# A decoder layer on one core: the weight products of cross-attention formed in the first stage

## Chip, core and metric

The kernel runs on one core of one Trainium2 chip. The metric is the time of one execution on the device, in microseconds (us), as the median of several runs. The core has a matrix engine (PE, which also loads its stationary operand), VectorE (DVE), ScalarE (ACT), GpSimd (POOL) and SyncE (SP, which here does nothing but issue transfers). Each has a queue of its own and runs it in order.

## What is computed

One decoder layer on 1024 tokens of width 1024: a token-mixing sub-layer (RWKV-7 and sparse attention side by side), cross-attention into 256 memory rows, and a gated feed-forward part, each followed by a residual sum and a layer norm. The change touches the second:

```python
def memory_cross_attention(x, mem, wq, wk, wv, wo):
    q = (x @ wq).reshape(B, S, X_HEADS, X_HEAD_DIM)      # 4 heads of 256
    k = (mem @ wk).reshape(B, M, X_HEADS, X_HEAD_DIM)    # 256 memory rows
    v = (mem @ wv).reshape(B, M, X_HEADS, X_HEAD_DIM)
    s = jnp.einsum('bhsd,bmhd->bhsm', q, k) * X_HEAD_DIM ** -0.5
    pr = jax.nn.softmax(s, axis=-1)
    o = jnp.einsum('bhsm,bmhd->bshd', pr, v).reshape(B, S, D_MODEL)
    return o @ wo
```

(axes reordered for reading). Since `q k^T = x (wq k^T)`, the product of `wq` with a head's keys can be formed without `x`; likewise `v wo` without the softmax.

## The kernel before

All arithmetic is in float32, each operand split into a high part and a low rest (`split`, lines 199 to 201: ScalarE copies the high part, VectorE subtracts), and each product is three PE products (`mm3`, lines 194 to 197). Weights come through `wload` (lines 211 to 229): units of 128 x 1024 numbers, 512 KB, go into a tile `raw` (one buffer in each pool) and are split into `wh` and `wl` (two buffers in each pool). In the first stage the two pools `wa` and `p0` take turns, so two units can be on their way and four can be held split.

First stage, in program order: the projection `nsa_proj(512, 512)`, then `mem_T` (the memory transposed and split), `mem_k(0)`, `mem_v(0)`, `windows` (reads back part of the projection, `ev`), `nsa_proj(1024, 280)`, `compress` (two weights of 2 units each), `mem_k(1)`, `windows`, `mem_v(1)`, `compress`, `mem_k(2)`, `nsa_proj(0, 512)`, `mem_v(2)`, `mem_k(3)`, `mem_v(3)`. `mem_k(j)` multiplies 256 columns of `xa_wk` with the memory and stores 2 tiles in a scratch tensor `kscr`; `mem_v` does the same for `vscr`. The projection copies each result tile to `nst` by ScalarE, GpSimd rotates some columns (lines 355 to 358), and SP stores it to `rawn` (line 359). All copies of this kind share four buffers (`stt`).

After that stage the weight pool is `wa` alone, for the RWKV part, whose first products are called `prj`. Cross-attention comes later: `x_query(h)` forms a head's queries (`xq`) and splits them, `kscr` and `vscr` are read back and split (`kvld`), `x_front` forms scores (`xs`) and softmax, `x_back` transposes the probabilities (`xpt`) and multiplies with the values (`xo`), and `out_proj` multiplies with `xa_wo` (`op`), adds the residual and normalises. Large tiles go into two pools by the letters of `PLAN` (m or a). The framework orders the instructions of each engine when it builds the kernel, by readiness and by program order, so that neighbours in the program can change places.

Of the kernel before, what the change touches and what calls it, by code (L numbers as in the profile page):

```python
# [10 lines left out]
F32 = mybir.dt.float32  # L11
# [31 lines left out]
PSPLIT = "ggv"  # L43
FILL = (1, 0.9, 0.95, 0.95, 0.95, 0.95, 0.95, 0.95)
FILL0 = 1
PLAN = "mmmmmmmm" "aaaa" "a" "aaaammmm" "mmmmaaaa" "aaaa" "aa" "mmmmaama" "mmaa" "a" "maaammmm" + "aaaam" * 5
LAG = 3
GT = 8
XQ = 3
L_DENSE = 0.69  # L50
L_SUBST = 42
L_BACK = 7
# [74 lines left out]
def layer_kernel(ctx: ExitStack, tc, I, out, cst):  # L127
# [22 lines left out]
    def stt(shape, dt=F32, name="st"):  # L150
        return cur["st"].tile(shape, dt, tag="st", name=name, bufs=cur["nst"])
# [188 lines left out]
    def nsa_proj(cc, n, scale, nb, nh, w=None, ahead=lambda tt: None):  # L340
        w = w or wload([win[:, NSA0 + cc:NSA0 + cc + n]])
        for tt in range(NT):
            ahead(tt)
            ps = pg("np")
            gemmN(ps[:, :n], xT, tt, w, 0, n)
            t = stt([P, HALF], name="nst")
            S.activation(t[:, :n], ps[:, :n], AF.Copy, scale=scale)
            v = t[:, 0:256 * nb].rearrange("p (b h d) -> p b h d", h=4, d=64)[:, :, 0:nh, 0:16]
            for z in range(nb):
                vz = v[:, z]  # L350
                co = cso[:, tt * 16:tt * 16 + 16]
                si = cso[:, P + tt * 16:P + tt * 16 + 16]
                a = p0.tile([P, nh, 16], F32, name="rpa", tag="rpa", bufs=2)
                b = p0.tile([P, nh, 16], F32, name="rpb", tag="rpb", bufs=2)
                G.tensor_tensor(a, vz, bc(co, nh), op=OP.mult)
                G.tensor_tensor(b[:, :, 0:8], vz[:, :, 8:16], bc(si[:, 0:8], nh), op=OP.mult)
                G.tensor_tensor(b[:, :, 8:16], vz[:, :, 0:8], bc(si[:, 8:16], nh), op=OP.mult)
                G.tensor_tensor(vz, a, b, op=OP.add)
            SP.dma_start(rawn[tt * P:(tt + 1) * P, cc:cc + n], t[:, :n])

    rows_h = [slice(0, 64), slice(64, 128)]

# [79 lines left out]
                ms = slice(mt * P, mt * P + P)  # L442
                split(pt, memh[:, kh * 4:kh * 4 + 4, ms], meml[:, kh * 4:kh * 4 + 4, ms])

    def mem_k(j):
        w = wload([I["xa_wk"][0][:, j * 256:(j + 1) * 256]])
        for q in range(2):
            ps = pg("mk")
            for k in range(8):
                mm3(ps[:, :MEM], *w.at(k, q * P, P), memh[:, k], meml[:, k], k == 0, k == 7)  # L450
            t = stt([P, MEM], name="mks")
            S.activation(t, ps[:, :MEM], AF.Copy)
            SP.dma_start(kscr[j * 256 + q * P:j * 256 + q * P + P, :], t)

    def mem_v(j):
        w = wload([I["xa_wv"][0][:, j * 256:(j + 1) * 256]])
        for mt in range(2):
            ms = slice(mt * P, mt * P + P)
            ps = pg("mv")
            for k in range(8):  # L460
                mm3(ps[:, :256], memh[:, k, ms], meml[:, k, ms], *w.at(k, 0, 256), k == 0, k == 7)
            t = stt([P, 256], name="mvs")
            S.activation(t, ps[:, :256], AF.Copy)
            SP.dma_start(vscr[ms, j * 256:(j + 1) * 256], t)
# [24 lines left out]
    V.tensor_scalar(hbias, pv[:, c0:c0 + 8], 0.5, None, op0=OP.mult)  # L489

    mem_T()
    mem_k(0)
    mem_v(0)
    blocks = windows(512, "nsa_pe_k")
    nsa_proj(1024, 280, 1.0, 1, 2)
    compress(*blocks, "nsa_ck_w1", "nsa_ck_w2", True)
    mem_k(1)
    blocks_v = windows(640, "nsa_pe_v")
    mem_v(1)
    compress(*blocks_v, "nsa_cv_w1", "nsa_cv_w2", False)  # L500
    mem_k(2)
    nsa_proj(0, 512, 0.125, 2, 4)
    mem_v(2)
    mem_k(3)
    mem_v(3)


    gq = list(range(16))
# [836 lines left out]
            SP.dma_start(acc[i], src[i * 256:(i + 1) * 256, :].rearrange("(a p) d -> p a d", p=P))  # L1345
        return acc

    def out_proj(a, wname, res, gname, bname, dst=None, order=range(NT)):
        acc = residual(res, [tt // 2 for tt in order[::2]])
        norm = layer_norm(acc, gname, bname, dst)  # L1350
        nT = Act(b8, "nT")

        def add(w, j, tt):
            ps = pg("op")
            gemmN(ps, a, tt, w, 0, HALF)
            v = acc[tt // 2][:, tt % 2, j * HALF:(j + 1) * HALF]
            V.scalar_tensor_tensor(v, v, ALPHA, ps, op0=OP.mult, op1=OP.add)

        cols = lambda j: wload([I[wname][0][:, j * HALF:(j + 1) * HALF]])
        w = cols(0)  # L1360
        for tt in order:
            add(w, 0, tt)
        w = cols(1)
        rows = []
        for tt in range(NT + LAG):
            if tt < NT:
                add(w, 1, tt)
            if tt >= LAG:
# [6 lines left out]
    x1T, _ = out_proj(mT, "mix_w_o", x, "ln1_g", "ln1_b", x1, order=(4, 5, 6, 7, 0, 1, 2, 3))


    qh = [b8([P, 2, T], F32R, f"xqh{h}") for h in range(4)]
    ql = [b8([P, 2, T], F32R, f"xql{h}") for h in range(4)]
    def x_query(h):  # L1380
        w = wload([I["xa_wq"][0][:, h * 256:(h + 1) * 256]])
        for half in range(2):
            for q in range(2):
                ps = pg("xq")
                gemmT(ps, w, q * P, x1T, half)
                hs = slice(half * HALF, (half + 1) * HALF)
                split(ps, qh[h][:, q, hs], ql[h][:, q, hs])

    def x_front(h, half):
        ps = []  # L1390
        for q2 in range(2):
            s = pss("xs").rearrange("p (q m) -> p q m", m=MEM)
            for q in range(2):
                ts_ = slice((half * 4 + 2 * q2 + q) * P, (half * 4 + 2 * q2 + q + 1) * P)
                for k in range(2):
                    mm3(s[:, q], qh[h][:, k, ts_], ql[h][:, k, ts_], km[0][:, 2 * h + k], km[1][:, 2 * h + k], k == 0, k == 1)
            nm = sm.tile([P, 4], F32, name="xnm", tag="xnm", bufs=3)
            V.tensor_reduce(nm[:, 0:2], s, axis=AX.X, op=OP.max)
            V.tensor_scalar(nm[:, 0:2], nm[:, 0:2], -X_SCALE, None, op0=OP.mult)
# [6 lines left out]
        return ps  # L1406

    def x_back(h, half, ps):
        PT = []
        for mt in range(2):  # L1410
            pt = pst("xpt").rearrange("p (a t) -> p a t", t=P)
            for q in range(4):
                PE.transpose(pt[:, q, :], ps[q // 2][:, q % 2, mt * P:(mt + 1) * P], ident)
            PT.append([stt([P, HALF], F32R, name="xPT") for _ in range(2)])
            split(pt.rearrange("p a t -> p (a t)"), *PT[mt])
        for q in range(2):
            ps = pg("xo")
            for mt in range(2):
                ds_ = slice(h * 256 + q * P, h * 256 + q * P + P)
                mm3(ps, vm[0][:, mt, ds_], vm[1][:, mt, ds_], *PT[mt], mt == 0, mt == 1)  # L1420
            k = 2 * h + q
            split(ps, oT.h[half][k // 4][:, k % 4, :], oT.l[half][k // 4][:, k % 4, :])

    pend = []
    for h in range(XQ):
        x_query(h)
        if h == 0:
            kvh = [b8([P, 2048], F32R, f"kvh{i}") for i in range(2)]
            kvl = [b8([P, 2048], F32R, f"kvl{i}") for i in range(2)]
            for i in range(2):  # L1430
                t = b8([P, 2048], name="kvld")
                if i == 0:
                    SP.dma_start(t.rearrange("p (a m) -> p a m", m=MEM), kscr.rearrange("(a p) m -> p a m", p=P))
                else:
                    SP.dma_start(t.rearrange("p (a d) -> p a d", d=D), vscr.rearrange("(a p) d -> p a d", p=P))
                split(t, kvh[i], kvl[i])
            km = [kvh[0].rearrange("p (a m) -> p a m", m=MEM), kvl[0].rearrange("p (a m) -> p a m", m=MEM)]
            vm = [kvh[1].rearrange("p (a d) -> p a d", d=D), kvl[1].rearrange("p (a d) -> p a d", d=D)]
            oT = Act(b8, "oT")
# [12 lines left out]
    wup, wdn = I["ffn_w_up"][0], I["ffn_w_down"][0]
# [13 lines left out]
    for n in (2, 4, 4, 4, 4, 4):  # L1466
# [68 lines left out]
```

## Time and profile before

| | us |
|---|---|
| median of 3 runs (2221.66 to 2224.29) | 2224.1 |
| the profiled execution, its own time | 2223.49 |
| its span, first to last instruction | 2221.7 |
| PE busy with products | 2131.7 (96%) |
| VectorE busy | 1232.4 (55%) |
| ScalarE busy | 889.2 (40%) |
| GpSimd busy | 475.0 (21%) |

Busy shares are averages over stages with different limits. A record of a PE product overlaps the next ones, so a busy PE is not PE at its peak: the distance between starts tells the rate. A row of the timeline gives start, duration, engine, line, operation, output and inputs; what stands in brackets at its end is the idle time before it and what ended that. L195, L196 and L197 are the three products of `mm3`, L200 and L201 the two halves of a split, L224 the load of a weight unit, and SPq is SP's queue.

### The profile page before, as it was taken

What the parts mean: (1) busy time and instruction counts of PE and PEld (TensorE: products, weight loads), DVE (VectorE), ACT (ScalarE), POOL (GpSimd) and SP (SyncE); (2) the same over time, 40 slices, a digit from 0 to 9 for tenths busy, and PEclk for the clock granted to TensorE, in tenths of its full rate; (3) what the DMA queues carried; (4) which work ended last, traced back from release to release, by engine and by line L of the source; (5) the groups of instructions that cost most, each with busy time, mean ns of one, the idle gap of its engine ahead of it and who ended that gap; (6) DMA issues with size and microseconds to landing.
All of it is one profiled execution on the core that took longest, in us unless ns stands there. A gap on an engine that the chain in (4) does not pass through costs nothing.

```text
span 2221.7 us, 31651 instructions
## 1 busy us (share of the span) xinstructions
PE 2131.7 (96%) x12301; PEld 1706.0 (77%) x12301; DVE 1232.4 (55%) x2416; ACT 889.2 (40%) x1441; POOL 475.0 (21%) x544
## 2 busy tenths in 40 slices
PE   9989999999999899999899999999999999999997
PEld 7978777777778667756678877788888888888886
DVE  3422576777652787888656535275444434344447
ACT  3433443544533576776523424142322313132232
POOL 2112231333300244444422101030100101000013
PEclk9999999999999999999999999999999999999999
DMA  6544112121223321112252313111111111111102
GB/s 206 152 150 124 49 24 56 36 52 32 62 59 94 110 66 45 42 45 68 72 189 86 123 38 114 39 39 57 38 48 48 54 42 57 39 57 57 57 29 86
DMA packets 196659, 157.91 MB, mean 71 GB/s; under 512 B 49061, under 2 KB 164766, under 8 KB 196510
## 3 DMA queue, kind: packets, MB, share of 16 engines
q1 hardware_dynamic: 184798, 139.10, 21.2%
q10 hardware_dynamic: 11136, 14.68, 2.0%
q0 software_dynamic: 576, 2.10, 0.3%
q8 instruction: 98, 1.61, 0.3%
q14 instruction: 51, 0.42, 0.1%
HBM read 125.86 MB, written 29.98 MB: 70 GB/s over the span
## 4 chain that ended last, share of the span: by engine, by line
PE 47%; DVE 5%; ACT 2%; DMA 1%; issue 1%; POOL 0%; SPq 0%; ACTq 0%; DVEq 0%; POOLq 0%
PE up L196 7%; PE up L197 7%; PE up L195 7%; PE dn L195 4%; PE dn L197 4%; PE dn L196 4%; PE op L195 2%; PE op L197 1%; PE op L196 1%; PE xq L195 1%; PE xq L196 1%; PE xq L197 1%; DVE acc L1334 1%; ACT acc L1333 1%; DVE bs L1327 1%
## 5 line engine op out<-in xcount | busy, mean ns | idle before, releaser
L200 ACT ACTIVATE wh<-raw 128x1024 fp32r<-128x1024 f32 (+1 forms) x160 | 168.8, 1055 | 474.9 <-PE dn L197 138.1
L201 DVE TENSOR_TENSOR wl<-raw,wh 128x1024 fp32r<-128x1024 f32 (+1 forms) x160 | 198.1, 1239 | 282.5 <-ACT wh L200 281.5
L196 PE MATMUL up<-nTl,wh 128*128 128x512 f32 x704 | 276.5, 393 | 0.0
L197 PE MATMUL up<-nTh,wl 128*128 128x512 f32 x704 | 276.4, 393 | 0.0
L195 PE MATMUL up<-nTh,wh 128*128 128x512 f32 x704 | 276.4, 393 | 0.0
L1458 DVE SCALAR_TENSOR_TENSOR cv<-up,pv,cv 128x511 f32<-128x511 f32 (+1 forms) x176 | 131.5, 747 | 145.4 <-ACT cv L1456 143.4
L1482 POOL TENSOR_TENSOR cv<-cv 128x512 f32<-128x512 f32 x44 | 56.8, 1291 | 630.9 <-DVE cl L1462 413.5
L196 PEld LDWEIGHTS up<-nTl,wh 128*128 128x128 f32 x704 | 132.3, 188 | 29.6
L195 PEld LDWEIGHTS up<-nTh,wh 128*128 128x128 f32 x704 | 132.2, 188 | 29.6
L197 PEld LDWEIGHTS up<-nTh,wl 128*128 128x128 f32 x704 | 132.2, 188 | 29.6
L1106 POOL TENSOR_TENSOR pl<-pe,ph 128x512 fp32r<-128x512 f32 x87 | 114.3, 1317 | 161.3 <-ACT ph L1105 97.3
L195 PE MATMUL dn<-wh,gT 128*128 128x512 f32 x352 | 138.1, 393 | 0.2 <-ACT wh L200 0.2
L197 PE MATMUL dn<-wh,gT 128*128 128x512 f32 x352 | 137.5, 391 | 0.0
L196 PE MATMUL dn<-wl,gT 128*128 128x512 f32 x352 | 136.9, 389 | 0.0
L1493 DVE SCALAR_TENSOR_TENSOR acc<-acc,dn 128x512 f32<-128x512 f32 x96 | 65.5, 686 | 95.5 <-PE dn L197 94.9
L1456 ACT ACTIVATE cv<-up,pv 128x512 f32<-128x512 f32 x88 | 68.5, 778 | 117.2 <-PE up L197 117.2
L195 PE MATMUL gt<-xTh,wh 128*128 128x512 f32 x256 | 113.0, 441 | 0.5 <-DVE nm L1074 0.5
L197 PE MATMUL gt<-xTh,wl 128*128 128x512 f32 x256 | 102.3, 399 | 0.0
L196 PE MATMUL gt<-xTl,wh 128*128 128x512 f32 x256 | 101.9, 398 | 0.0
L1335 POOL TENSOR_TENSOR acc<-acc,lngb 128x1024 f32<-128x1024 f32 x21 | 50.4, 2401 | 206.0 <-DVE acc L1334 129.8
L1105 ACT ACTIVATE ph<-pe 128x512 fp32r<-128x512 f32 (+1 forms) x148 | 90.2, 627 | 6.9 <-POOL macc L1223 4.6
L195 PE MATMUL prj<-xTh,wh 128*128 128x512 f32 x208 | 90.5, 435 | 2.2 <-ACT wh L200 2.2
(365 smaller groups left out, 5092.2 us busy)
## 6 DMA issues: line engine op xcount, KB each, us to landing
raw<-in_ffn_w_up_dram SPq DMA_DIRECT2D x88, 256.0 KB
raw<-in_w_in_dram SPq DMA_DIRECT2D x33, 512.0 KB
raw<-in_ffn_w_down_dram SPq DMA_DIRECT2D x22, 512.0 KB
gscr<-gst ACTq DMA_DIRECT2D x32, 256.0 KB
rawn<-nst SPq DMA_DIRECT2D x16, 256.0 KB
raw<-in_xa_wk_dram SPq DMA_DIRECT2D x8, 512.0 KB
raw<-in_xa_wv_dram SPq DMA_DIRECT2D x8, 512.0 KB
gl<-gscr SPq DMA_DIRECT2D x16, 256.0 KB
```

Source lines behind the costliest of these rows:

```text
L195: PE.matmul(o, lh, rh, start=start, stop=False)
L196: PE.matmul(o, lh, rl, start=False, stop=False)
L197: PE.matmul(o, ll, rh, start=False, stop=stop)
L200: S.activation(h, src, AF.Copy)
L201: V.tensor_sub(l, src, h.bitcast(F32))
L1105: S.activation(h, e, AF.Copy)
L1106: in_turn("l", LTURN)(l, e, h.bitcast(F32), op=OP.subtract)
L1335: (V if tt == NT - 1 else G).tensor_tensor(r[:, c], r[:, c], gb[:, 1, c], op=OP.add)
L1456: S.activation(c, ps, AF.Identity, scale=pc("cw2", ci), bias=pc("ffn_conv_b", ci))
L1458: V.scalar_tensor_tensor(c[:, s:], ps[:, :HALF - s], pc(nme, ci), c[:, s:], op0=OP.mult, op1=OP.add)
L1482: G.tensor_tensor(c[0], c[0], c[1], op=OP.mult)
L1493: V.scalar_tensor_tensor(v, v, 1.0 if f else ALPHA, ps, op0=OP.mult, op1=OP.add)
```

## The change

The products `xa_wq k^T` (per head 1024 x 256) and `v xa_wo` (256 x 1024) are formed in the first stage and stored in larger `kscr` and `vscr` (4 MB each). Cross-attention multiplies `x1T` with the first to get scores, transposes the probabilities into `PT`, and multiplies these with the second in `out_proj`. The queries, the value product and the reading back and splitting of keys and values go. `mem_k` and `mem_v` are each split in two: `mem_head` forms a head's keys or values and leaves them split on the chip, and the new `mem_k` and `mem_v` multiply them with `xa_wqT` (transposed by the host, as `xT` is) or `xa_wo`. Stores of `rawn` are issued by GpSimd, those of `kscr` and `vscr` by ScalarE. `PLAN` and the parameter `XQ` follow.

```diff
-PLAN = "mmmmmmmm" "aaaa" "a" "aaaammmm" "mmmmaaaa" "aaaa" "aa" "mmmmaama" "mmaa" "a" "maaammmm" + "aaaam" * 5
+PLAN = "mmmmmmmm" "aaaa" "a" "aaaammmm" "mmmmaaaa" "aaaa" "a" "mmmmmmmm" + "a" * 25
-            SP.dma_start(rawn[tt * P:(tt + 1) * P, cc:cc + n], t[:, :n])
+            G.dma_start(rawn[tt * P:(tt + 1) * P, cc:cc + n], t[:, :n])
...
-    def mem_k(j):
-        w = wload([I["xa_wk"][0][:, j * 256:(j + 1) * 256]])
+    def mem_head(wname, j):
+
+        w = wload([I[wname][0][:, j * 256:(j + 1) * 256]])
+        h, l = (p0.tile([P, 2, MEM], F32R, tag=f"mh{i}", name="mh", bufs=2) for i in range(2))
         for q in range(2):
             ps = pg("mk")
             for k in range(8):
                 mm3(ps[:, :MEM], *w.at(k, q * P, P), memh[:, k], meml[:, k], k == 0, k == 7)
-            t = stt([P, MEM], name="mks")
-            S.activation(t, ps[:, :MEM], AF.Copy)
-            SP.dma_start(kscr[j * 256 + q * P:j * 256 + q * P + P, :], t)
+            split(ps[:, :MEM], h[:, q], l[:, q])
+        return h, l
+
+    def mem_k(j, h, l):
+
+        w = wload([I["xa_wqT"][j * 256:(j + 1) * 256, :]], kt=2)
+        for d in range(4):
+            ps = pg("kw")
+            for z in range(2):
+                for k in range(2):
+                    mm3(ps[:, z * MEM:(z + 1) * MEM], *w.at(k, (2 * d + z) * P, P), h[:, k], l[:, k], k == 0, k == 1)
+            t = stt([P, 2, MEM], name="kws")
+            S.activation(t.rearrange("p z m -> p (z m)"), ps, AF.Copy)
+            S.dma_start(kscr[d * 256:(d + 1) * 256, j * MEM:(j + 1) * MEM].rearrange("(z p) m -> p z m", p=P), t)
+
+    def mem_v(j, h, l):
+
+        w = wload([I["xa_wo"][0][j * 256:(j + 1) * 256, :]], kt=2)
         for mt in range(2):
             ms = slice(mt * P, mt * P + P)
+            for o in range(2):
+                ps = pg("vw")
+                for k in range(2):
+                    mm3(ps, h[:, k, ms], l[:, k, ms], *w.at(k, o * HALF, HALF), k == 0, k == 1)
+                t = stt([P, HALF], name="vws")
+                S.activation(t, ps, AF.Copy)
+                S.dma_start(vscr[j * MEM + mt * P:j * MEM + mt * P + P, o * HALF:(o + 1) * HALF], t)
...
+    heads = lambda j: (mem_head("xa_wk", j), mem_head("xa_wv", j))
+    hk, hv = heads(0)
     blocks = windows(512, "nsa_pe_k")
+    mem_k(0, *hk)
     nsa_proj(1024, 280, 1.0, 1, 2)
+    mem_v(0, *hv)
     compress(*blocks, "nsa_ck_w1", "nsa_ck_w2", True)
-    mem_k(1)
+    hk, hv = heads(1)
     blocks_v = windows(640, "nsa_pe_v")
-    mem_v(1)
+    mem_k(1, *hk)
+    mem_v(1, *hv)
+    hk, hv = heads(2)
     compress(*blocks_v, "nsa_cv_w1", "nsa_cv_w2", False)
-    mem_k(2)
+    mem_k(2, *hk)
+    mem_v(2, *hv)
+    hk, hv = heads(3)
     nsa_proj(0, 512, 0.125, 2, 4)
-    mem_v(2)
-    mem_k(3)
-    mem_v(3)
+    mem_k(3, *hk)
+    mem_v(3, *hv)
...
             for q in range(2):
-                    mm3(s[:, q], qh[h][:, k, ts_], ql[h][:, k, ts_], km[0][:, 2 * h + k], km[1][:, 2 * h + k], k == 0, k == 1)
+                gemmN(s[:, q], x1T, half * 4 + 2 * q2 + q, w, 0, MEM)
...
+            k = 2 * h + mt
+            split(pt.rearrange("p a t -> p (a t)"), PT.h[half][k // 4][:, k % 4, :], PT.l[half][k // 4][:, k % 4, :])
...
     for h in range(4):
+        w = wload([kscr[:, h * MEM:(h + 1) * MEM]])
         for half in range(2):
-            if half and h + XQ < 4:
-                x_query(h + XQ)
-            pend.append((h, half, x_front(h, half)))
-            if len(pend) > 1 + (h == 3):
+            pend.append((h, half, x_front(h, half, w)))
+            if len(pend) > 1:
                 x_back(*pend.pop(0))
     for a in pend:
         x_back(*a)
-    x2T, acc = out_proj(oT, "xa_wo", x1, "ln2_g", "ln2_b")
+    x2T, acc = out_proj(PT, vscr, x1, "ln2_g", "ln2_b")
```

## Rows read from the trace of the kernel before

**Rows 1.** Timeline of PE: start, duration, engine, line, operation, output and inputs.

```profile
24.45 0.39 PE L197 MATMUL np<-wh,xTl 128*128 128x512 f32 x1
...
34.87 0.39 PE L197 MATMUL np<-wh,xTl 128*128 128x512 f32 x1
...
95.00 0.28 PE L195 MATMUL cm<-wh,blkh 128*126 128x256 f32 x1
...
139.53 0.40 PE L195 MATMUL np<-wh,xTh 128*128 128x512 f32 x1
...
184.72 0.28 PE L195 MATMUL mv<-wh,memh 128*128 128x256 f32 x1
...
190.43 0.29 PE L195 MATMUL mk<-memh,wh 128*128 128x256 f32 x1
...
206.03 0.50 PE L197 MATMUL prj<-xTh,wl 128*128 128x512 f32 x1 [0.53 <-DVE wl L201]
...
1227.26 1.03 PE L244 MATMUL toT<-ident,acc 128*128 128x128 f32 x8
1228.05 0.48 PE L195 MATMUL xq<-nTh,wh 128*128 128x512 f32 x1
...
1385.19 0.40 PE L195 MATMUL op<-wh,oTh 128*128 128x512 f32 x1
```

**Rows 2.** Windows: busy us by engine (PE, PEld, DVE, ACT, POOL), clock, DMA share, GB/s.

```profile
100.00:140.00 40.00, 30.60 (x229) 27.27 (x230) 21.78 (x29) 21.38 (x33) 0.00 (x0) 1.00 0.57 175
```

**Rows 3.** Waits of PE from 100 to 140: total, times, longest.

```profile
PE cm L196 <- DVE wl L201: 3.2, 5, 0.9
```

**Rows 4.** Timeline of SP's queue, weight loads of one of the two buffers.

```profile
97.98 0.39 SPq L224 DMA_DIRECT2D raw<-in_xa_wk_dram  x1
...
113.52 1.84 SPq L224 DMA_DIRECT2D raw<-in_nsa_cv_w_dram  x2
...
119.67 0.37 SPq L224 DMA_DIRECT2D raw<-in_nsa_cv_w_dram  x1
...
145.06 3.53 SPq L224 DMA_DIRECT2D raw<-in_xa_wv_dram  x2
```

**Rows 5.** Timeline of ScalarE, the unit loaded at 113.52.

```profile
117.33 1.06 ACT L200 ACTIVATE wh<-raw 128x1024 fp32r<-128x1024 f32 x1 [0.28 <-DMA raw<-in_nsa_cv_w_dram]
```

**Rows 6.** Products by tile: count, ns min/median/max, first and last start.

```profile
L195 PE MATMUL xq<-nTh,wh x128: 389/393/628, 1228.0 to 1339.4; 128*128 128x512 f32 x128
...
L195 PE MATMUL xs<-kvh,xqh x64: 277/283/387, 1270.6 to 1367.6; 128*128 128x256 f32 x64
...
L195 PE MATMUL xo<-xPT,kvh x32: 389/396/793, 1340.1 to 1384.5; 128*128 128x512 f32 x32
```

**Rows 7.** Groups by line, 1260 to 1390: busy us, mean ns, idle before.

```profile
L1398 DVE TENSOR_REDUCE xnm<-xs 128x2 f32<-128x512 f32 x16 | 10.9, 688 | 29.1 <-PE xs L197 29.0
```

**Rows 8.** Timeline of SP's queue around the end of the first projection.

```profile
57.30 0.34 SPq L359 DMA_DIRECT2D rawn<-nst  x1
60.47 1.19 SPq L378 DMA_DIRECT2D ev<-rawn  x2
61.79 1.04 SPq L224 DMA_DIRECT2D raw<-in_w_in_dram  x2
```

**Rows 9.** By tile `kld`: a transfer that GpSimd issues, issue ns and landing.

```profile
L979 POOL DMA_DIRECT2D kld<-rawn x2: 882/976/1071, 717.0 to 724.1; - x2
...
DMA to landing us min/median/max: 5.1/5.8/6.5
```

**Rows 10.** By tile `nst` and `gst`: ScalarE's copies and its DMA issues, ns.

```profile
L347 ACT ACTIVATE nst<-np x24: 378/598/599, 16.1 to 185.1; 128x512 f32<-128x512 f32 x16, 128x280 f32<-128x280 f32 x8
...
L548 ACTq DMA_DIRECT2D gscr<-gst x32: 326/326/348, 260.9 to 809.2; - x32
```

**Rows 11.** Waits of SP's queue from 0 to 210: total, times, longest.

```profile
SPq L359 <- POOL nst L358: 37.7, 21, 3.1
SPq L224 <- DVE wl L201: 33.6, 25, 2.4
```

More of the change, by code (lines that the diff above doesn't have):

```diff
@@ L45 @@
 FILL0 = 1
-PLAN = "mmmmmmmm" "aaaa" "a" "aaaammmm" "mmmmaaaa" "aaaa" "aa" "mmmmaama" "mmaa" "a" "maaammmm" + "aaaam" * 5
+PLAN = "mmmmmmmm" "aaaa" "a" "aaaammmm" "mmmmaaaa" "aaaa" "a" "mmmmmmmm" + "a" * 25
 LAG = 3
 GT = 8
-XQ = 3
 L_DENSE = 0.69
@@ L420, in compress @@
                 S.activation(VC[64:127, g, 0:64], ps[0:63, 0:64], AF.Copy)
-    kscr = drp.tile([D, MEM], F32, name="kscr")
-    vscr = drp.tile([MEM, D], F32, name="vscr")
+    kscr = drp.tile([D, 4 * MEM], F32, name="kscr")
+    vscr = drp.tile([4 * MEM, D], F32, name="vscr")
     memh = p0.tile([P, 8, MEM], F32R, name="memh")
@@ L450, in mem_k @@
                 mm3(ps[:, :MEM], *w.at(k, q * P, P), memh[:, k], meml[:, k], k == 0, k == 7)
-            t = stt([P, MEM], name="mks")
-            S.activation(t, ps[:, :MEM], AF.Copy)
-            SP.dma_start(kscr[j * 256 + q * P:j * 256 + q * P + P, :], t)
-    def mem_v(j):
-        w = wload([I["xa_wv"][0][:, j * 256:(j + 1) * 256]])
+            split(ps[:, :MEM], h[:, q], l[:, q])
[12 more added lines that the diff above has]
+        w = wload([I["xa_wo"][0][j * 256:(j + 1) * 256, :]], kt=2)
         for mt in range(2):
             ms = slice(mt * P, mt * P + P)
[L459 to L464, printed above, removed]
+            for o in range(2):
[5 more added lines that the diff above has]
+                S.dma_start(vscr[j * MEM + mt * P:j * MEM + mt * P + P, o * HALF:(o + 1) * HALF], t)
     def first(tt):
@@ L491, in layer_kernel @@
     mem_T()
-    mem_k(0)
-    mem_v(0)
+    heads = lambda j: (mem_head("xa_wk", j), mem_head("xa_wv", j))
+    hk, hv = heads(0)
     blocks = windows(512, "nsa_pe_k")
+    mem_k(0, *hk)
     nsa_proj(1024, 280, 1.0, 1, 2)
+    mem_v(0, *hv)
     compress(*blocks, "nsa_ck_w1", "nsa_ck_w2", True)
-    mem_k(1)
+    hk, hv = heads(1)
     blocks_v = windows(640, "nsa_pe_v")
-    mem_v(1)
+    mem_k(1, *hk)
+    mem_v(1, *hv)
+    hk, hv = heads(2)
     compress(*blocks_v, "nsa_cv_w1", "nsa_cv_w2", False)
-    mem_k(2)
+    mem_k(2, *hk)
+    mem_v(2, *hv)
+    hk, hv = heads(3)
     nsa_proj(0, 512, 0.125, 2, 4)
-    mem_v(2)
-    mem_k(3)
-    mem_v(3)
+    mem_k(3, *hk)
+    mem_v(3, *hv)
     gq = list(range(16))
@@ L1346, in residual, with out_proj @@
         return acc
-    def out_proj(a, wname, res, gname, bname, dst=None, order=range(NT)):
+    def out_proj(a, weight, res, gname, bname, dst=None, order=range(NT)):
         acc = residual(res, [tt // 2 for tt in order[::2]])
@@ L1357, in add @@
             V.scalar_tensor_tensor(v, v, ALPHA, ps, op0=OP.mult, op1=OP.add)
-        cols = lambda j: wload([I[wname][0][:, j * HALF:(j + 1) * HALF]])
+        cols = lambda j: wload([weight[:, j * HALF:(j + 1) * HALF]])
         w = cols(0)
@@ L1374, in layer_kernel, with x_front @@
     x1 = drp.tile([T, D], F32, name="x1")
[L1375 to L1389, printed above, removed]
+    x1T, _ = out_proj(mT, I["mix_w_o"][0], x, "ln1_g", "ln1_b", x1, order=(4, 5, 6, 7, 0, 1, 2, 3))
+    PT = Act(b8, "PT")
+    def x_front(h, half, w):
         ps = []
@@ L1393, in x_front @@
             for q in range(2):
-                ts_ = slice((half * 4 + 2 * q2 + q) * P, (half * 4 + 2 * q2 + q + 1) * P)
-                for k in range(2):
-                    mm3(s[:, q], qh[h][:, k, ts_], ql[h][:, k, ts_], km[0][:, 2 * h + k], km[1][:, 2 * h + k], k == 0, k == 1)
+                gemmN(s[:, q], x1T, half * 4 + 2 * q2 + q, w, 0, MEM)
             nm = sm.tile([P, 4], F32, name="xnm", tag="xnm", bufs=3)
@@ L1408, in x_back @@
     def x_back(h, half, ps):
-        PT = []
         for mt in range(2):
@@ L1413, in x_back @@
                 PE.transpose(pt[:, q, :], ps[q // 2][:, q % 2, mt * P:(mt + 1) * P], ident)
[L1414 to L1422, printed above, removed]
-    pend = []
[L1425 to L1439, printed above, removed]
+            k = 2 * h + mt
+            split(pt.rearrange("p a t -> p (a t)"), PT.h[half][k // 4][:, k % 4, :], PT.l[half][k // 4][:, k % 4, :])
+    pend = []
     for h in range(4):
+        w = wload([kscr[:, h * MEM:(h + 1) * MEM]])
         for half in range(2):
-            if half and h + XQ < 4:
-                x_query(h + XQ)
-            pend.append((h, half, x_front(h, half)))
-            if len(pend) > 1 + (h == 3):
+            pend.append((h, half, x_front(h, half, w)))
+            if len(pend) > 1:
                 x_back(*pend.pop(0))
@@ L1511 @@
         'rwkv_r_k', 'rwkv_gn_g', 'rwkv_gn_b', 'nsa_pe_k', 'nsa_pe_v', 'nsa_ck_w1', 'nsa_ck_w2', 'nsa_cv_w1',
-        'nsa_cv_w2', 'merge_p_a', 'merge_p_b', 'mix_w_o', 'ln1_g', 'ln1_b', 'xa_wq', 'xa_wk', 'xa_wv', 'xa_wo',
+        'nsa_cv_w2', 'merge_p_a', 'merge_p_b', 'mix_w_o', 'ln1_g', 'ln1_b', 'xa_wk', 'xa_wv', 'xa_wo',
         'ln2_g', 'ln2_b', 'ffn_w_up', 'ffn_conv_w', 'ffn_conv_b', 'ffn_w_down', 'ln3_g', 'ln3_b']
@@ L1527 @@
     aps["xT"] = nc.dram_tensor("in_xT_dram", (D, T), F32, kind="ExternalInput").ap()
+    arrays["in_xa_wqT_dram"] = np.ascontiguousarray(np.asarray(inputs["xa_wq"])[0].T)
+    aps["xa_wqT"] = nc.dram_tensor("in_xa_wqT_dram", (D, D), F32, kind="ExternalInput").ap()
     arrays["in_const_dram"] = shape_constants()
```

## The prediction

> **What bounds the kernel now.** I read the page's slices first: the matrix engine (PE) shows as busy nearly everywhere. That share hides small waits, since a record of a 256-column product lasts 0.28 us while the next one starts 0.12 us later; so I count starts in the timeline of PE, not busy time. 45 starts of 512-column products take 10.42 us, 0.232 each; 48 of 256 columns take 5.71, 0.119 each [rows 1]. PE time goes with columns, and a narrow product is not dearer per column.
>
> Then the two stages that the change touches, by the points at which they begin and end [rows 1]. First stage: from the end of the 280-column projection (95.0) to the second 512-column projection (139.5) PE does 240 products of 256 and some 3 us of small ones: 32 us of work in 44.5. Its waits there end with a weight split [rows 3]. In the rest of the stage it runs almost without gaps, but for about 4 us in the tail after 184.7.
>
> What makes the splits late is the round trip of a weight buffer. `wload` brings units of 512 KB in turn into two buffers called `raw`, one in each of two pools; a buffer is free when both halves of its split are done. A unit is issued at 113.52 [rows 4], ScalarE starts on it at 117.33 and takes 1.06 [rows 5], VectorE follows, and the same buffer's next load goes at 119.67: a round trip R of 6.15 us with nothing in its way. Over the seven trips of this buffer from 97.98 to 145.06 [rows 4] the mean is 6.7, since gelu table loads and the splitting of `blk` lie between. Each R of both buffers yields a pair of units. A pair feeds 48 products of 256 (5.7 us), in `compress` only 24 (2.9 us). This stretch is bound by R, not by PE.
>
> **What the change does to cross-attention.** Removed: 384 products of 512 (`xq`), 192 of 256 (`xs`), 96 of 512 (`xo`); the rows show one of three like lines each [rows 6]. 480 x 0.232 + 192 x 0.119 = 134 us. Added: scores straight from `x1T` against the folded weight, 4 heads x 8 row tiles x 8 k x 3 = 768 products of 256 = 91.8 us. The 64 transposes stay, 8.3 us at 0.13 (eight take 1.03 [rows 1]), as do some 32 of the layer norm before, 4.2 us. The stage ran from 1228.05 to 1385.19 [rows 1], 157.1 us: 147 of work and 10 of waits and short clock dips. After: 104.3 of work plus waits. Most old waits stood between query, score and value products and go. Late next is the last softmax (reduce 0.69 [rows 7], exponentials, multiply, split, some 4 us as an estimate), of which the transposes of the half before and the first output products cover a part; and the second pair of output weights, whose split starts when the last scores release their buffer. I take 4 us of waits (2 to 7): 108.3, so **-48.8** (-50.8 to -45.8). The loads per head are as many units as before, over 23 us of PE, so hidden; the two loads `kvld` and their splits lay beside `xq` and are worth nothing. Three of the four residual loads now take slots that `x1T` frees, 11 us ahead of the output projection, which needs a new one every 11 us: hidden too. If not, a load of 1 MB late costs a few us.
>
> **What it does to the first stage.** The head products are the old `mk` and `mv` work. Added per head: 48 products of 256 (5.7 us) and 24 of 512 (5.6 us), 45 us over four heads: PE work is hardly saved, it is moved. But 16 more units must pass the two buffers. By parts:
>
> (a) Up to the end of the 280-column projection stand two `mem_head` and `mem_k(0)` in place of `mem_k` and `mem_v`: +5.7. The `rawn` stores now come from GpSimd. By SP, the store at 57.30 let the dependent `ev` load go at 60.47 [rows 8]. GpSimd's DMA issues in this trace take 0.98 us and land 5.8 after issue [rows 9]. So `ev` waits until about 64, and behind it on SP wait the two units of `mem_k(0)`, where now two units go at 61.79 [rows 8]. They finish splitting at 71.5 to 73, and PE wants them at 70. I take +2.5 (0, if the build puts them ahead of `ev`, to 4.5).
>
> (b) From there to the second 512 projection: 15 pairs (`mem_v(0)`, 4 of `compress`, 6 of `mem_head`, 2 of `mem_k`, 2 of `mem_v`), the first there in time, so 14 round trips. PE's work is 77 us and 14 R is 86 to 102, so R sets the time: 0.5 us to the first free buffer, 14 R, and 4.3 us of products after the last unit, 4.8 + 14 R against 44.5 before. For R: what lengthened seven trips by 0.55 each (two gelus, one `blk`) comes no more often in fourteen, so 6.4. Then ScalarE, which stands in the trip, gets per pair some 1.5 us more: 20 copies at 0.60 and 12 head splits at 0.38, by the two widths of the `nst` copy, and 20 DMA issues at 0.33 [rows 10], over 15 pairs; they run in order, so a copy that waits for PE holds a landed unit. And 5 MB of stores share DMA engines that are busy to 0.57 here already [rows 2]. No row shows that together; it lies between 6.25 (all in ScalarE's idle time) and 7.3 (the mean of 6.7 plus 0.6). I take 6.85, nearest to the measured mean: 100.7, **+56.2** (+47.8 to +62.5).
>
> (c) The 512 projection: as before. (d) The tail from 184.72 to 206.03 [rows 1], three groups of products with 4 us of waits, 21.3 us, becomes `mem_k(3)` and `mem_v(3)`, 11.3 us and 1 us of waits (0 to 2): **-9.0**.
>
> Stores taken off SP: SP waited 37.7 us for GpSimd before it could store a tile, and 33.6 for VectorE's split before a weight load [rows 11]. In the bound stretch the loads follow the split (above), so the queue's order is not what delays them: value 0. If it were, R would drop, and the first rival gains. The Trainium skill's DMA: Bandwidth & Descriptors (Issuing engines are not separate DMA queues) says that DMAs from several engines run on the same 16 engines, and that spreading them saves only the sequencer's time to issue; that speaks against this part of the change. By it SP saves some 40 issues of 0.33 us, at most 13 us that SP has to spare, and the sum stays.
>
> Sum: 5.7 + 2.5 + 56.2 - 9.0 = +55.4 in the first stage, -48.8 in cross-attention: **+6.6 us**. The profiled execution took 2223.5 us (its span 2221.7), 0.6 under the median of 2224.1: 2230.1 on it, 2230.7 on the median; I say 2230.5.
>
> **Rivals.**
> *The loads keep pace* (faster). Net is 14 R - 92.8 + (waits in a and d): with 2.5 and 1 it turns at R = 6.4, without them at 6.6. For it: the quiet trip of 6.15, and the folded weights' units have rows of 4 KB instead of 1 KB. Against: the measured mean of 6.7, with less on ScalarE than there will be. With R = 6.25, no waits in (a) and (d) and 50.8 saved: -7.3 + rounding, 2216 to 2217 us. Chance 0.20.
> *A wash.* R about 6.4: the two stages exchange some 49 us for 49, 2224 us. Chance 0.20.
> *GpSimd's stores hold the projection up.* A `nst` tile is free when its store lands. With four buffers and 3.1 us of PE per tile of the 280 projection this decides from a life of 12.4 us; worked out it is 0.4 (copy) + 0.9 (rope) + 1.0 + 5.8 = 8.1. At 16 us it costs eight tiles x 0.9 = 7 us and delays `ev` by as much: 2241 to 2245 us. Chance 0.06.
> *Cross-attention doesn't give what it says.* If each of eight groups of scores waited for its softmax, some 3.5 us each, 28 us of the gain would go: 2258. Against: per group of 11.5 us PE has two reduces of 0.69 [rows 7] and little more on each other engine. Chance 0.04.
>
> **How the numbers follow.** My forecast (R from 6.5 to 7.3) has 0.50. A measurement of this kernel tells about 0.2% (4.4 us) from no change. Of the 0.50 some 0.08 lie under +4.4. Slower: 0.42 + 0.10 = 0.52; same 0.08 + 0.20 = 0.28; faster 0.20. The range goes from the first rival, 2216, to the upper bounds of the sum, +64.7 and -45.8, 2243; it leaves out the last rival and the tails of two others.
>
> **What would show it.** From the first `xs` to the first steady `op` product about 108 us; over 115, and my price there is wrong. The second 512 projection should start about 64 us later than 139.5, the steady `prj` about 55 later than 206.0. Same-buffer weight loads between should lie 6.9 us apart; at 6.3 it is the first rival. SP's waits for `nst` vanish and those for VectorE's split grow. If PE waits for a `nst` copy, it is GpSimd's stores. Between 206 and cross-attention, and from the output projection on, all should only be shifted; any gain or loss there would prove the sum incomplete.

## The result, and the profile after

| | median, us | runs | ratio to before (95%) |
|---|---|---|---|
| before | 2223.4 | 6 (2221.7 to 2224.3) | 1 |
| changed | 2237.8 | 6 (2235.2 to 2248.2) | 1.0072 (1.0052 to 1.0091) |

The change makes the kernel slower by 14.4 us. The forecast was +6.6, 2230.5 us, with a range of 2216 to 2243. Direction and range hold; the size is off by 7.3 us (2237.8 less 2230.5), as a change 14.4 for 6.6. The two profiled executions have spans of 2221.7 and 2236.2 us, so the traces show the same 14.5.

The points at which the stages begin stand in the timeline of PE after the change (start, duration, engine, line, operation, output and inputs; in brackets the idle time before and its end). Lines have moved: L194 to L196 are the three products, L199 and L200 the two halves of a split, L223 the load of a weight unit.

```profile
81.80 0.40 PE L194 MATMUL np<-wh,xTh 128*128 128x280 f32 x1 [1.74 <-ACT wh L199]
...
103.12 0.39 PE L194 MATMUL vw<-wh,mh 128*128 128x512 f32 x1
...
210.74 0.39 PE L194 MATMUL np<-wh,xTh 128*128 128x512 f32 x1
...
256.06 0.28 PE L194 MATMUL kw<-mh,wh 128*128 128x256 f32 x1
...
271.62 0.51 PE L194 MATMUL prj<-xTh,wh 128*128 128x512 f32 x1 [3.96 <-ACT wh L199]
...
272.88 0.79 PE L196 MATMUL prj<-xTh,wl 128*128 128x512 f32 x1 [0.53 <-DVE wl L200]
...
1295.79 0.37 PE L194 MATMUL xs<-wh,nTh 128*128 128x256 f32 x1
...
1401.26 0.48 PE L195 MATMUL op<-wl,PTh 128*128 128x512 f32 x1
```

They are the landmarks of [rows 1]. Subtracting neighbours gives the ledger; the last column is x2, the experiment below in which SP issues all stores (its difference to before, too):

| part | before | predicted change | changed | x2 |
|---|---|---|---|---|
| (a) up to the end of the 280-column projection | 95.0 | +8.2 | +8.1 | +8.6 |
| (b) to the second 512 projection | 44.5 | +56.2 | +63.1 | +55.0 |
| (c) the 512 projection | 45.2 | 0 | +0.1 | +0.9 |
| (d) the tail | 21.3 | -9.0 | -4.5 | -7.2 |
| middle, to the first `xs` | 1022.0 | 0 | +0.9 | |
| cross-attention | 157.1 | -48.8 | -51.7 | |
| from the output projection on | | 0 | -1.6 | |

So the missing 8 us lie in (b), 6.9, and (d), 4.5, less 2.9 that cross-attention gave beyond the forecast. The -1.6 at the end is not a gain there: 13 output products are done at its landmark, against 3 before. Where in (b) shows in SP's queue, the loads of one buffer, beside those of [rows 4]:

```profile
142.16 4.55 SPq L223 DMA_DIRECT2D raw<-in_xa_wk_dram  x2
150.93 0.37 SPq L223 DMA_DIRECT2D raw<-in_xa_wv_dram  x1
157.78 0.37 SPq L223 DMA_DIRECT2D raw<-in_nsa_cv_w_dram  x1
```

From 142.16 to 150.93 are 8.77 us, to the next 6.85. Twelve such trips, from 114.30 to 202.39, have a mean of 7.34, where the forecast took 6.85. Put into its own formula, 4.8 + 14 x 7.34 = 107.6; the trace shows 210.74 - 103.12 = 107.6. The model of the stretch was right, and the one number in it that no row of before showed was too small. That it meets the trace to 0.1 us is luck: in the six other traces with two buffers, below, the same formula lies up to 3.2 us off.

One long trip, in ScalarE's rows of the same time (ACTq are the DMA issues of ScalarE):

```profile
141.44 0.38 ACTq L465 DMA_DIRECT2D kscr<-kws  x1
141.86 1.20 ACT L464 ACTIVATE kws<-kw 128x512 f32<-128x512 f32 x2 [0.45 <-PE kw L196]
142.52 0.93 ACTq L465 DMA_DIRECT2D kscr<-kws  x2
...
144.13 0.37 ACTq L465 DMA_DIRECT2D kscr<-kws  x1
148.59 1.06 ACT L199 ACTIVATE wh<-raw 128x1024 fp32r<-128x1024 f32 x1 [3.54 <-DMA raw<-in_xa_wk_dram]
```

The unit issued at 142.16 is split at 148.59, after ScalarE had waited 3.54 us for it: 6.4 us on its way, beside four stores issued between 141.44 and 144.13. Before, a unit took 3.8, from 113.52 [rows 4] to 117.33 [rows 5]. The other trip of 8.77 (185.32 to 194.09) has the same 6.4.

The DMA packets tell more of the load of 142.16. Here are packets, MB and share of the 16 engines' time by queue, from 143.35 to 145.85 and from there to 147.60; q1 carries SP's transfers and q10 ScalarE's (in x2, where SP issues all stores, q10 moves nothing in (b)):

```profile
q1 hardware_dynamic: 494, 0.49, 65.3%
q10 hardware_dynamic: 129, 0.12, 16.1%
...
q10 hardware_dynamic: 659, 0.64, 103.4%
q1 hardware_dynamic: 21, 0.02, 3.4%
```

The unit is 512 packets of 1 KB. By 145.85, 3.7 us after its issue, all but about a sixteenth of them are through; the rest trickle, 21 packets in 1.75 us, while ScalarE's stores move 659. In this trace sixteen packets of 4 bytes end each load: fifteen stand at 145.47 to 145.81, the last at 148.13, and the split starts at 148.59. The loads of 185.32 and 194.09 (6.0 us) end in the same way, most of the sixteen at the usual time and the last 1.2 to 1.9 us later, beside packets of q10.

SP's waits up to 275 (total, times, longest), to be held against [rows 11]:

```profile
SPq L223 <- DVE wl L200: 134.4, 39, 34.3
SPq L377 <- DMA rawn<-nst: 20.9, 4, 8.4
...
SPq L1030 <- DMA rawn<-nst: 6.0, 1, 6.0
SPq L398 <- PE kc L408: 5.2, 1, 5.2
```

As foretold, the waits for `nst` copies are gone and those for splits have grown (34.3 of the 134.4 are one wait during the 512 projection, when no unit is needed). But new ones stand in the same queue: reads of `rawn` (L377 the blocks, L1030 `gr`) wait until GpSimd's stores have landed, and weight loads queue behind them. At 111.39 `gr` goes after 6.0 us of waiting, and the last unit of `nsa_ck_w` goes behind it, at 112.78.

The windows of PE (busy us of PE, PEld, DVE, ACT, POOL; granted clock; DMA share; GB/s) show one thing more; [rows 2] had 1.00 and 0.57:

```profile
103.12:140.00 36.88, 31.31 (x210) 27.64 (x209) 20.75 (x29) 18.64 (x28) 2.19 (x5) 0.95 0.55 182
140.00:210.74 70.74, 58.94 (x375) 53.60 (x373) 26.93 (x29) 31.83 (x47) 0.00 (x0) 0.90 0.62 199
```

The granted clock is at the lower of its two levels (1.2 instead of 2.4 GHz) for part of the stretch; a mean of 0.90 is 20% of 70.7 us at the half. For one fall of it, at 156.55, PE had waited 1.41 us before the product at 150.18 and 1.97 before the one at 156.54.

### The profile page after: what moved, and what is told of

Its sections match the earlier page's. It is cut to its first block, busy times and chain, and to the rows that moved or that the text cites. A ratio compares the mean times of both kernels' runs of the same rounds, so it can differ in the third digit from the quotient of the medians.

```text
span 2236.2 us, 32456 instructions
## 1 busy us (share of the span) xinstructions
PE 2138.0 (96%) x12685; PEld 1729.9 (77%) x12685; DVE 1231.9 (55%) x2414; ACT 902.0 (40%) x1453; POOL 487.1 (22%) x568
## 4 chain that ended last, share of the span: by engine, by line
PE 45%; DVE 4%; ACT 1%; DMA 1%; issue 1%; POOL 1%; SPq 0%; ACTq 0%; DVEq 0%; POOLq 0%
PE up L195 7%; PE up L196 7%; PE up L194 7%; PE dn L194 4%; PE dn L196 4%; PE dn L195 3%; PE op L194 1%; PE op L196 1%; PE op L195 1%; PE xs L196 1%; PE xs L195 1%; PE xs L194 1%; DVE acc L1353 1%; ACT acc L1352 1%; DVE bs L1346 1%
## 5 line engine op out<-in xcount | busy, mean ns | idle before, releaser
L200 DVE TENSOR_TENSOR wl<-raw,wh 128x1024 fp32r<-128x1024 f32 (+1 forms) x176 | 217.6, 1239 | 304.5 <-ACT wh L199 277.8
L199 ACT ACTIVATE wh<-raw 128x1024 fp32r<-128x1024 f32 (+1 forms) x176 | 185.1, 1054 | 462.7 <-PE dn L196 138.4
L196 PE MATMUL up<-nTh,wl 128*128 128x512 f32 x704 | 276.4, 393 | 0.0
L194 PE MATMUL up<-nTh,wh 128*128 128x512 f32 x704 | 276.3, 393 | 0.0
L196 PEld LDWEIGHTS up<-nTh,wl 128*128 128x128 f32 x704 | 132.2, 188 | 29.6
L194 PEld LDWEIGHTS up<-nTh,wh 128*128 128x128 f32 x704 | 132.2, 188 | 29.6
L194 PE MATMUL dn<-wh,gT 128*128 128x512 f32 x352 | 138.1, 393 | 0.1
L196 PE MATMUL dn<-wh,gT 128*128 128x512 f32 x352 | 137.5, 391 | 0.0
L194 PE MATMUL gt<-xTh,wh 128*128 128x512 f32 x256 | 112.6, 440 | 0.5 <-DVE nm L1093 0.5
L196 PE MATMUL gt<-xTh,wl 128*128 128x512 f32 x256 | 102.2, 399 | 0.0
L194 PE MATMUL prj<-xTh,wh 128*128 128x512 f32 x208 | 91.0, 438 | 4.0 <-ACT wh L199 4.0
```

Of the source, the lines that this page charges most:

```text
L194: PE.matmul(o, lh, rh, start=start, stop=False)
L196: PE.matmul(o, ll, rh, start=False, stop=stop)
L199: S.activation(h, src, AF.Copy)
L200: V.tensor_sub(l, src, h.bitcast(F32))
```

## Experiments

Times stand against the changed kernel (2237.8, measured in the first session alone) or against before (2223.4; measured again in every session, the same within 2 us).

### Cross-attention alone

**x1_cross_only**: the kernel before with the new cross-attention, which takes `xa_wq` and `xa_wo` where the change has the formed products; the edit as against before, in part:

```diff
+    PT = Act(b8, "PT")
...
+                gemmN(s[:, q], x1T, half * 4 + 2 * q2 + q, w, 0, MEM)
...
+        w = wload([I["xa_wq"][0][:, h * MEM:(h + 1) * MEM]])
...
+    x2T, acc = out_proj(PT, I["xa_wo"][0], x1, "ln2_g", "ln2_b")
```

> The changed cross-attention on the first stage of before; the scores multiply with xa_wq and the last product with xa_wo instead of the folded weights (same shapes and loads), so the values are not the reference's. By my sum the stage alone gains 48.8 us and nothing else moves: 2223.4 - 48.8 = 2174.6; by the trace of the changed kernel, whose stage is 51.6 us shorter, 2171 to 2173. If scores waiting for their softmax or for weights had cost something that the first stage only hid, it would be above 2185.

Measured: 2171.0 us, ratio 0.9756 (0.9740 to 0.9773), so -53.0. The stage gives what it was priced at and 4 more: the trace of the changed kernel shows one wait of PE in it, 1.1 us, where I had taken 4. The rival in which cross-attention doesn't give falls, and with it any explanation of the loss there: the first stage alone costs 2237.8 - 2171.0 = 66.8 us, the +66.9 that the timeline shows.

### Who issues the stores

**x2_all_stores_on_sp** undoes that part of the change alone; **x5_rawn_on_sp** takes its first line, **x6_products_on_sp** the two others.

```diff
-            G.dma_start(rawn[tt * P:(tt + 1) * P, cc:cc + n], t[:, :n])
+            SP.dma_start(rawn[tt * P:(tt + 1) * P, cc:cc + n], t[:, :n])
...
-            S.dma_start(kscr[...], t)
+            SP.dma_start(kscr[...], t)
...
-                S.dma_start(vscr[...], t)
+                SP.dma_start(vscr[...], t)
```

> All stores of the first stage issued by SP again (rawn, kscr, vscr), the rest as changed. Theory A (the round trip of two weight buffers, lengthened by the stores' share of the DMA engines): who issues matters little, 2232 to 2241 us, round trips still about 7.3 us. Theory B (GpSimd's late landings and ScalarE's issues hold up weight loads and splits): 2225 to 2230, round trips about 6.7. Theory C (SP's order was the old bound, and the change freed it): slower, 2245 or more.

> Only the rawn stores go back to SP; the product stores stay with ScalarE. The move of all stores to other engines was worth 10 us against the change (2237.8 and 2227.4). Theory G (GpSimd's stores: they land late, SP waits for them before it reads back, and weight loads wait behind): 2228 to 2231, the wait of the gate reads gone, first compress weights 2 to 3 us earlier. Theory S (ScalarE's stores: a second ring beside the loads, and ScalarE held by store buffers): 2234 to 2237.

> Only the product stores go back to SP; rawn stays with GpSimd. Theory S: 2228 to 2231, no weight load takes over 5 us to land beside product stores, the clock in the stretch is back at 1.00 since no wait is over 2 us. Theory G: 2234 to 2237. If both add: about 2232 here and in the run beside it.

| | median, us | ratio to before (95%) | against the changed kernel |
|---|---|---|---|
| x2, all on SP | 2227.4 | 1.0015 (1.0006 to 1.0025) | -10.4 |
| x5, `rawn` on SP | 2234.0 | 1.0055 (1.0036 to 1.0074) | -3.8 |
| x6, products on SP | 2231.6 | 1.0034 (1.0022 to 1.0046) | -6.2 |

The 10.4 are clear; they are more than the 7.3 that the forecast missed, and most of the loss. x2 is what Theory B expected, and excludes A and C. The two halves add up to 10.0; that each is worth its own part is less sure, since x5's interval overlaps that of the changed kernel. The windows of (b) in x5, then in x6:

```profile
101.93:208.60 106.67, 89.35 (x583) 80.63 (x581) 47.45 (x58) 50.40 (x74) 1.61 (x4) 0.92 0.61 194
106.22:209.04 102.82, 88.09 (x583) 78.65 (x581) 46.05 (x58) 49.79 (x74) 2.19 (x5) 0.93 0.63 204
```

So (b) gains 0.9 us in x5 and 4.8 in x6, where both together (x2) gain 8.1; trips average 7.19 and 7.23, against 6.87 for both. The marks were hit in part. In x5 the blocks' reads wait 3.5 us in place of 20.9, but `gr` still waits 4.3 of its 6.0. In x6 the clock is 0.93 and not 1.00 (PE's longest wait is 4.0 us), and three loads take 5.0 to 5.5 us: less than 6.4, but not under 5. The windows of x2:

```profile
103.56:140.00 36.44, 30.78 (x221) 27.38 (x220) 20.71 (x30) 19.41 (x29) 1.62 (x4) 1.00 0.60 183
140.00:203.06 63.06, 53.64 (x365) 46.37 (x363) 25.35 (x29) 30.34 (x46) 0.00 (x0) 1.00 0.69 224
249.19:263.26 14.07, 12.45 (x76) 10.25 (x74) 3.68 (x3) 8.07 (x12) 3.87 (x14) 1.00 0.76 246
```

The stretch takes 203.06 - 103.56 = 99.5 us, for which the forecast had said 100.7, at a granted clock of 1.00 throughout. Its twelve trips from 114.82 to 197.22 have a mean of 6.87, the forecast's 6.85. What SP does there, at the place shown above for the changed kernel, and ScalarE's splits of the two units:

```profile
141.54 0.43 SPq L223 DMA_DIRECT2D raw<-in_xa_wk_dram  x1
142.01 1.90 SPq L465 DMA_DIRECT2D kscr<-kws  x2
144.32 0.37 SPq L223 DMA_DIRECT2D raw<-in_xa_wk_dram  x1
145.79 3.19 SPq L478 DMA_DIRECT2D vscr<-vws  x4
149.07 0.41 SPq L223 DMA_DIRECT2D raw<-in_xa_wv_dram  x1
```

```profile
146.60 1.06 ACT L199 ACTIVATE wh<-raw 128x1024 fp32r<-128x1024 f32 x1 [0.34 <-DMA raw<-in_xa_wk_dram]
...
149.38 1.06 ACT L199 ACTIVATE wh<-raw 128x1024 fp32r<-128x1024 f32 x1 [0.75 <-DMA raw<-in_xa_wk_dram]
```

Both units take 5.06 us from issue to split (141.54 to 146.60, 144.32 to 149.38), and ScalarE waits well under 1 us for each, though stores stand between the loads in SP's queue. The same transfers run; only who issues them, and so when and in which queue, differs.

### What of ScalarE's stores it is

**x3_no_product_stores** leaves nearly all of these stores out:

```diff
-            S.dma_start(kscr[...], t)
+            if j == 0:
+                S.dma_start(kscr[...], t)
...
-                S.dma_start(vscr[...], t)
+                if j < 0:
+                    S.dma_start(vscr[...], t)
```

> The products are formed and copied, but only the first head's keys are stored; cross-attention reads that one for all heads and the output product reads xa_wo, so the values are not the reference's. 7 of 8 MB of stores are gone. Theory A: round trips fall from 7.3 to 6.4 to 6.6 us, the stretch from the 280-column projection to the second 512-column one from 107.6 to about 96 us, and the tail by 4: 2222 to 2226 us. If it is the moved products themselves, or a slow clock after waits, that cost the time: 2234 to 2238.

Measured: 2231.3 us, ratio 1.0030 (1.0016 to 1.0043), -6.5. The expectation missed: without the stores the stretch is still 101.4 us and the trips 7.08. To have no such stores is worth no more than to have SP issue them (x6, -6.2), so their bytes as such cost next to nothing; what cost was that they ran from ScalarE. The clock of that stretch is 0.93, hardly above the 0.92 of the changed kernel, and (b) is 6.2 us shorter all the same. In x3 `rawn` still comes from GpSimd: `gr` goes at 112.67 and the weight unit behind it at 114.06.

**x10_eight_store_buffers** gives the copies eight buffers instead of four, so that no copy of ScalarE waits for an earlier store to land.

```diff
-    cur.update(st=p0, nst=4, b8=p0, n8=3, w=[wa, p0])
+    cur.update(st=p0, nst=8, b8=p0, n8=3, w=[wa, p0])
```

> The change with eight store buffers in the first stage in place of four, GpSimd and ScalarE still issuing. The product stores on ScalarE cost about 6 us against SP, the rawn stores on GpSimd about 4. If ScalarE is held because a copy waits for a store to land and free its buffer, with splits queued behind: 2229 to 2233, the tail's 4 us wait ahead of prj gone. If it is the stores' own ring beside the loads, or GpSimd's landings that SP waits for: 2235 to 2239.

Measured: 2238.6 us, ratio 1.0070 (1.0055 to 1.0085): nothing. The wait that I suspected is real in one place. ScalarE in the tail of the changed kernel:

```profile
269.46 0.60 ACT L477 ACTIVATE vws<-vw 128x512 f32<-128x512 f32 x1 [2.56 <-DMA kscr<-kws]
269.49 0.93 ACTq L478 DMA_DIRECT2D vscr<-vws  x2
270.51 1.06 ACT L199 ACTIVATE wh<-raw 128x1024 fp32r<-128x1024 f32 x1 [0.46 <-DMA lw<-in_rwkv_w_dram]
```

A copy waits 2.56 us for a store buffer, the split of the next stage's first unit stands behind it, and `prj` waits 3.96 us. With eight buffers no copy in the tail waits for a store, `prj` still waits 2.25 us, and nothing is gained over the whole, so store buffers are not the cause.

**x9_heads_late** forms the head products of heads 1 and 2 directly ahead of their second product, not one product earlier.

```diff
-    hk, hv = heads(1)
+    mem_k(1, *mem_head("xa_wk", 1))
...
-    mem_k(1, *hk)
-    mem_v(1, *hv)
-    hk, hv = heads(2)
+    mem_v(1, *mem_head("xa_wv", 1))
...
-    mem_k(2, *hk)
-    mem_v(2, *hv)
+    mem_k(2, *mem_head("xa_wk", 2))
+    mem_v(2, *mem_head("xa_wv", 2))
```

> The change with the head products of heads 1 and 2 directly ahead of the product that uses them, not one early; loads and work are the same in number. If the round trip of the weight buffers sets the stretch, the order of pairs changes little: 2234 to 2242. If the early split hides the wait for the split of a head's product (about 1.5 us, four times), it is 2242 to 2246.

Measured: 2237.4 us, ratio 1.0072 (1.0052 to 1.0092). Being one product early buys nothing here: in (b) of x9 PE waits for the splits of units, and never for the split of a head.

### The round trip

If two weight buffers set the stretch, a third must shorten it, in the kernel before too. **x4_three_buffers** and **x7_before_three_buffers** put two `raw` into `p0` beside the one in `wa`, used in turn; **x8_three_buffers_all_sp** is x4 with SP's stores, **x11_four_buffers_all_sp** has a fourth, **x12_three_sp_six_stores** is x8 with six store buffers.

```diff
-    cur.update(st=p0, nst=4, b8=p0, n8=3, w=[wa, p0])
+    cur.update(st=p0, nst=4, b8=p0, n8=3, w=[wa, p0], r=[wa] + [p0] * 2)
...
-            raw = wp.tile([P, ku, n], F32, tag="raw", bufs=1, name="raw")
+            rw = in_turn("r", cur["r"]) if "r" in cur else wp
+            raw = rw.tile([P, ku, n], F32, tag="raw", bufs=2 if rw is p0 else 1, name="raw")
...
+    cur.pop("r")
```

> A third weight buffer in the first stage (two in p0, one in wa, in turn), all else as changed. Theory A: three loads on their way, so the stretch is no longer bound by the round trip but by PE (77 us) and the DMA engines: 107.6 falls to 85 to 92, total 2216 to 2223 us. Theory B (issue order and landings) or PE work as the cause: under 5 us, 2233 to 2238.

> The kernel before with a third weight buffer in the first stage and nothing else. If the round trip bound this stretch already there: the 12.5 us of waits from 95 to 139.5 and some 3 of the tail fall to 2 to 5 in all, 2210 to 2215 us. If PE waits for something else there: 2220 to 2224.

> The change with three weight buffers and all stores on SP. With the third buffer alone it took 2210.7. If the issuing engines cost as much here as with two buffers (10 us): 2201 to 2204. If three loads on their way cover such delays: 2206 to 2212. If SP's queue, now with loads behind stores, holds them up: above 2212.

> Four weight buffers, all stores on SP. With three it took 2206.5 and the stretch 85 us, of which 77 were my count of PE work and 6 waits. If loads still set part of it: 2202 to 2205. If PE and the engines' order are what is left: 2205 to 2208.

> Three weight buffers, all stores on SP, six store buffers instead of four. If copies still wait for stores there: 2202 to 2205; if not: 2205 to 2208.

| | median, us | ratio to before (95%) | (b), us |
|---|---|---|---|
| x7, before, three | 2211.3 | 0.9941 (0.9918 to 0.9965) | 35.7 (44.5 with two) |
| x4, changed, three | 2210.7 | 0.9939 (0.9925 to 0.9954) | 89.4 (107.6 with two) |
| x8, changed, three, all on SP | 2206.5 | 0.9925 (0.9906 to 0.9944) | 85.1 (99.5 with two) |
| x11, the same, four | 2204.3 | 0.9926 (0.9907 to 0.9945) | 83.9 |
| x12, three, six stores | 2207.2 | 0.9932 (0.9917 to 0.9947) | 86.4 |

One buffer more takes 27 us from the changed kernel, more than expected, and 12 from the one before, as expected. With three buffers SP's stores are worth 4.2 us (x8 against x4), less than with two, and the intervals overlap. The stretch in x8, as a window, and PE's waits in it:

```profile
101.61:186.67 85.06, 79.78 (x583) 74.31 (x581) 47.64 (x59) 53.86 (x78) 2.64 (x4) 0.98 0.76 246
```

```profile
PE hT L402 <- ACT hid L397: 2.2, 2, 1.2
PE cm L194 <- ACT wh L199: 1.1, 1, 1.1
PE cm L195 <- DVE wl L200: 0.9, 1, 0.9
PE mk L194 <- ACT wh L199: 0.5, 1, 0.5
```

85.1 us against the 77 of PE's work that the forecast counts, and waits for splits of 3 us in all: the stretch is nearly PE's again, although the DMA engines are busy to 0.76. With (b) 18, 9 and 14 us shorter in x4, x7 and x8, that shows the round trip as the bound. With enough buffers the fold comes out even with the kernel before, treated alike: x4 0.6 us under x7, x8 4.8 under it, within the intervals in both cases. That is near what PE's work allows: 45 us of products more in the first stage against 51.7 us less in cross-attention, 7 us at best. x8, x11 and x12 beat both kernels as they were, with two buffers, and can't be told apart: neither a fourth weight buffer nor more store buffers shows a gain.

## Why the prediction was right or wrong

- **What bounds the stage: right.** The two-buffer trip, not PE, sets (b): shown by x4, x7 and x8, and, within 3.2 us, by 4.8 + 14 R with the measured R (107.6 for 107.6, in x2 101 for 99.5, in x6 106 for 102.8).
- **The range held in part by luck.** (b) with +63.1 and (d) with -4.5 both lie above their upper bounds, +62.5 and -8.0; cross-attention lies below its lower one, -51.7 for -50.8, and makes up for 2.9 us.
- **"Stores taken off SP ... value 0": the step that failed.** I argued that loads follow the split, so that SP's order doesn't delay them, and allowed only a gain. The mirror case was left out: that stores issued elsewhere, with no place in the loads' queue, can make the trip longer. Undone it is worth 10.4 us (x2), 6.2 for ScalarE's stores and 3.8 for GpSimd's. In the sum this is mostly R, 7.34 instead of 6.85 over fourteen trips, 6.9 us; the rest is in (d). The halves are less sure than the whole.
- **R itself: right for the kernel with SP's stores.** 6.87 in x2. What I had added for copies and head splits on ScalarE was about right; the changed kernel came out at the upper bound of 7.3, "the mean of 6.7 plus 0.6".
- **(a): right in sum, wrong in one reason.** +8.1 for +8.2. GpSimd's issue and landing were taken from `kld`, 0.98 and 5.8 us [rows 9]; `rawn`'s own row after the change says 0.58 and a median of 2.4, the first `ev` goes at 60.47 as before, and the wait (1.74 at 81.80) comes later. `kld` was the wrong neighbour: it reads 512 KB at a time, where `rawn`'s stores write at most 256 KB.
- **GpSimd's stores as a rival: right place, wrong price.** I had them hold up the projection through `nst` buffers, from a life of 12.4 us; no product waits for them. They hold up SP: 20.9 us of waits ahead of the blocks' reads and 6.0 ahead of `gr`, with weight loads behind.
- **(d): mis-sized,** -4.5 for -9.0. Of the 4.5 missing, 3.0 are the wait of `prj`, 3.96 where I took 1 us; with SP's stores it is 0.98 and (d) is -7.2.
- **Cross-attention: right, and undersized by 3 to 4 us.** 105.5 us for 108.3; 13 of the output products are done by then, against 3 before. (768 x 0.119 is 91.4, where the sum has 91.8.)
- **The loads keep pace, a wash:** both asked for R of about 6.4, 6.6 at most; the trace has 7.34, and x2 6.87.

**What stays open** is a part of why a store that ScalarE issues costs a load more than the same store issued by SP. x3 and x10 exclude its bytes and its buffers. The traces show where: the last packets of a load run beside ScalarE's stores, and the split waits for them. Of the loads of (b) whose landing ScalarE waited for, the slowest took 6.4 us in the changed kernel, 6.8 in x5 and 6.2 in x10, where ScalarE issues the stores, and 5.4, 5.2 and 5.5 in x2, x3 and x6, where it issues next to none. One of x9, with 6.5 us, ran beside no store, so this is not the only way to land late. The Trainium skill's DMA: Bandwidth & Descriptors (Queues, rings and completion order) says that SP and ScalarE each own a queue row and that each DMA engine takes turns between the rows that have work; a load would then share every engine with stores that SP's own row would have put ahead of it or behind it. The packets agree with that so far as they go: they don't tell the engines apart, and no run here isolates it. How much of the 6.2 us these landings make, and how much the order of ScalarE's own work, isn't shown either. By the Trainium skill's rule on the same page (Issuing engines are not separate DMA queues), which the prediction weighed, spreading the issue saves only the time to issue; here it cost 10.4 us.

Nor could the clock's part be separated: at 0.95 and 0.90 over 36.9 and 70.7 us the lower level takes at most 1.8 + 7.1 us of full-speed time, and less where PE would have waited anyway. It isn't all of it, since x3 and x6 gain 6.2 and 4.8 us in (b) at 0.93; and in x9, at 0.87 over 109.1 us, some 5 us more at the lower level go with a (b) only 1.5 us longer.

## What to carry to other kernels

Where a stage lives on the round trip of a few load buffers, compute the stage as trips times R, and spend the first effort on another buffer: here it is worth 12 us before the change and 27 after it, where the change by itself loses 14. Don't value moving a store to another engine at zero because its old queue had time to spare; ask whose transfers it will then run beside, and who waits for its landing in an in-order queue. Work moved from one stage to another is paid there in what bounds that stage: here in round trips for 16 more units, not in PE's time.

## What the runs showed of the hardware that was not expected

GpSimd's stores of `nst` tiles after the change (issue in ns, then landing):

```profile
L358 POOL DMA_DIRECT2D rawn<-nst x24: 581/581/733, 32.3 to 259.4; - x24
...
DMA to landing us min/median/max: 2.1/2.4/5.7
```

An issue by GpSimd costs 0.58 us here against 0.33 for one by ScalarE [rows 10], and these stores land sooner than the 5.8 of `kld` [rows 9]. A 512 KB load took 3.8 us from issue to split with a quiet queue, 5.06 with stores of its own queue between, and 6.4 beside stores from ScalarE, where about a sixteenth of it came some 2 us after the rest. And the granted clock fell to a mean of 0.90 in a stretch whose longest wait of PE was 3.4 us, while it stayed at 1.00 in x2, whose waits reached 1.7, and in (b) before the change, whose waits reached 1.6.
